# One Trainium2 core, two-layer decoder: the head of the program in another order, with constant products while memory is loaded

## The chip, the cores and the metric

The kernel runs on one core of one Trainium2 chip. The metric is the device time of one execution in microseconds (us). The engines are TensorE (PE, its weight loads listed apart as PEld), VectorE (DVE), ScalarE (ACT), GpSimd (POOL) and SyncE (SP), which issues most of the transfers.

## The reference

Two decoder layers over 1024 positions of width 1024, then a final norm. Layer 0 mixes with latent attention (`mla_mixer`), layer 1 with a sliding window (`swa_mixer`). In both, four memory heads run beside the mixer. What the head of the program computes of this is cut out here:

```python
mem_n = rmsnorm(mem, mem_norm_g)                  # mem: 256 x 1024
kv = (mem_n @ w_mem_kv[i])                        # both layers i, 1024 x 512 each
hn = rmsnorm(x, attn_norm_g[0])                   # x: 1024 x 1024
proj = hn @ w_in                                  # 1024 x 928: c_q 384, c_kv 256, k_r 32, q_cross 256
c_q, c_kv = rmsnorm(c_q, ...), rmsnorm(c_kv, ...)
k_rope = rope(k_r, positions)                     # sines and cosines of positions
```

## The kernel before

Every f32 product is made of three products of rounded halves: `split` (L96) writes the high part on ScalarE (`AF.Copy`, L99, or with a gain as scale, L102) and the rest on VectorE (L100 or L103), and a product of `a` and `b` is `ah*bh + ah*bl + al*bh`. So each tile that TensorE uses has passed through ScalarE and then VectorE.

The head, in the order of the text (L503 to L665):

- The two tiles of `mem` (128 x 1024 each, 512 KB) are loaded first on SyncE (L510), then `w_mem_kv` of both layers in four chunks each (`wm0`, `wm1`, L329), then x tiles 0 and 1 (L533), `w_in` in eight row blocks (L563) and further x tiles.
- `mem_T` (L464) transposes memory on TensorE (`psTm`, L473) and splits it into `memTh`, `memTl`. A `between` call puts the copy of the memory gains (`gcol`, L166) between the two tiles.
- `MemProj.mul(c)` (L331) splits one chunk of a layer's weights (`wmh`, `wml`) and multiplies it: 12 products of 128 x 512 (L342 to L344) into `psmk`, 48 for each layer.
- `mem_root` (L477) computes the norm factors of a memory tile: a square with sum on ScalarE (L179), a square root (L187), and one Newton step of five small VectorE operations (L188 to L192).
- `a_N(t)` does the same for x tile t, multiplies it by its factor into one of two places of `fa0` (called y0, y1, y2 below; L209), and issues the load of x tile t+2 into the place that this frees. `a_T(t)` transposes y (`psT_a`, L216) and splits it into `xhls`.
- `w_in` is split into `wih` and `wil` (128 x 928, eight times).
- `rope_tables` (L236) computes the angles on VectorE (tiles `rt`), two Sins on ScalarE (L289, L291), and `cosb` on VectorE (L292, L293).
- The loop at L639 then runs over the eight x tiles: transpose of tile k, norm of k+1, input projection of k-1 (`a_in`, tile `psin`, 48 products: eight steps of six, L117 to L120), transposes of the result of k-2 (`a_cT`, `psct`, L631 and L632).

`a_in` reads its PSUM tile with seven operations: two squares, three scaled copies (L619 to L621), and the four multiplies of `rope` (L308 to L311) that need the sine and cosine tables. The `psin` tiles have two PSUM buffers, so `psin2` is written into the one that `psin0` used.

Which instruction comes next on an engine is set at build time by a scheduler that follows priorities, the dependences and its own costs. On the chip each engine runs its row in order. `tc.issue_after(i)`, which the change uses, keeps what stands under it from being put into a row before instruction i.

## Time and profile before

| what | value |
|---|---|
| runs | 2111.02, 2110.83, 2110.26 us; median 2110.83 |
| profiled execution | 2109.36 us, of it the span 2107.5 us |
| TensorE busy | 2082.1 us (99% of the span) |
| VectorE, ScalarE busy | 1476.6 us (70%), 1114.6 us (53%) |
| TensorE's waits in the first 200 us | 4.6 us for memory, 1.8 for `wml`, 0.6 for y2, some smaller |

A line of the timeline gives the start within the span, the duration, the engine, the line of the kernel, the operation, its output and inputs by name (numbers left out), their shapes and the count of like instructions that were joined. What stands in brackets is the idle time of the engine before it, and what ended it. "SPq" is a transfer issued by SyncE. Records of neighbouring products overlap: the pace is the difference of two starts, not the duration of one.

### The profile page before, as it was taken

The page shows a single profiled execution, that of the slowest core. Times are in us where ns is not written, and L with a number is a line of the kernel's source. Part 1 is how long each engine was busy: PE and PEld are TensorE (multiplying, and loading weights), DVE is VectorE, ACT ScalarE, POOL GpSimd, SP SyncE. Part 2 cuts the span into 40 slices and gives each one's busy share as a digit, 9 for nine tenths or more (in the row PEclk, how much of TensorE's full clock was granted, in tenths as well). Part 3 has the DMA queues.
Part 4 walks back from the last instruction along what each step waited for, and adds up shares of the span by engine and source line. Part 5 has one row for each costly group of instructions (what it writes and reads, how often), then busy time and mean ns, then how long its engine had stood idle before and what let it go on. Part 6 is the DMA issues. An engine that isn't in the chain of part 4 may idle for free.

```text
span 2107.5 us, 28961 instructions
## 1 busy us (share of the span) xinstructions
PE 2082.1 (99%) x9830; PEld 1691.0 (80%) x9830; DVE 1476.6 (70%) x2929; ACT 1114.6 (53%) x2408; POOL 147.9 (7%) x248
## 2 busy tenths in 40 slices
PE   8999999999999999999999999999999999999998
PEld 7888766678888888888888878778788888888887
DVE  8766677775977776976557535666977776976565
ACT  7554466656755444444445435776755444444453
POOL 1001001010000000000001133420000000000000
PEclk9999999999999999999999999999999999999999
DMA  6202223343355446954433634542345446844342
GB/s 237 79 1 76 63 64 92 91 136 100 112 169 165 152 143 231 321 152 156 136 119 103 153 90 126 140 136 85 111 164 165 159 141 231 318 150 154 119 120 88
DMA packets 180756, 292.34 MB, mean 139 GB/s; under 512 B 16659, under 2 KB 70784, under 8 KB 180608
## 3 DMA queue, kind: packets, MB, share of 16 engines
q1 hardware_dynamic: 174096, 272.07, 41.4%
q0 software_dynamic: 5200, 15.80, 2.1%
q10 hardware_dynamic: 1312, 2.63, 0.4%
q8 instruction: 77, 1.26, 0.3%
q14 instruction: 71, 0.58, 0.1%
HBM read 187.34 MB, written 81.18 MB: 127 GB/s over the span
## 4 chain that ended last, share of the span: by engine, by line
PE 90%; DVE 5%; DMA 2%; ACT 2%; issue 1%; SPq 0%; DVEq 0%; ACTq 0%
PE psy L1730 5%; PE psy L1728 5%; PE psy L1729 5%; PE psu L1421 5%; PE psu L1422 5%; PE psu L1423 5%; PE psz L1728 4%; PE psz L1730 4%; PE psz L1729 4%; PE psv L1422 4%; PE psv L1421 4%; PE psv L1423 4%; PE pso L947 4%; PE pss L917 3%; PE pswo L108 3%; PE pswo L110 3%
## 5 line engine op out<-in xcount | busy, mean ns | idle before, releaser
L927 ACT ACTIVATE p<-pss 128x512 f32<-128x512 f32 (+2 forms) x144 | 68.7, 487 | 69.2 <-DVE pss L925 52.5
L1728 PE MATMUL psy<-g 128*128 128x512 f32 x256 | 99.9, 390 | 0.0
L1729 PE MATMUL psy<-g 128*128 128x512 f32 x256 | 99.6, 389 | 0.0
L1730 PE MATMUL psy<-g 128*128 128x512 f32 x256 | 99.4, 390 | 0.0
L99 ACT ACTIVATE g<-i 128x512 fp32r<-128x512 f32 x79 | 49.7, 629 | 92.5 <-PE psz L1729 46.0
L100 DVE TENSOR_TENSOR g<-i,g 128x512 fp32r<-128x512 f32 x79 | 55.6, 704 | 47.6 <-ACT g L99 47.6
L99 ACT ACTIVATE i<-mr 128x512 fp32r<-128x512 f32 x78 | 47.8, 628 | 74.0 <-PE psy L1729 25.6
L796 DVE TENSOR_REDUCE m<-psx 128x1 f32<-128x1024 f32 (+7 forms) x96 | 72.0, 752 | 20.1 <-PE psx L795 19.7
L99 ACT ACTIVATE uh<-i 128x512 fp32r<-128x512 f32 x66 | 41.7, 631 | 83.9 <-PE psy L1729 39.5
L947 PE MATMUL pso<-p,vf 128*128 128x512 f32 (+2 forms) x192 | 85.4, 527 | 0.6 <-ACT p L927 0.6
L100 DVE TENSOR_TENSOR uh<-i,uh 128x512 fp32r<-128x512 f32 x66 | 45.6, 690 | 46.8 <-ACT uh L99 46.6
L1728 PE MATMUL psz<-g 128*128 128x512 f32 x192 | 74.7, 389 | 0.0
L1729 PE MATMUL psz<-g 128*128 128x512 f32 x192 | 74.7, 389 | 0.0
L1730 PE MATMUL psz<-g 128*128 128x512 f32 x192 | 74.7, 389 | 0.0
L1320 ACT ACTIVATE mr<-mr,gcol 128x256 f32<-128x256 f32 (+1 forms) x160 | 63.9, 475 | 13.5 <-DMA mr<-in_mlp_w_up_dram 13.5
L100 DVE TENSOR_TENSOR i<-mr,i 128x512 fp32r<-128x512 f32 x78 | 53.6, 687 | 21.5 <-ACT i L99 21.5
L917 PE MATMUL pss<-qh,kh 97*128 97x512 f32 (+2 forms) x144 | 67.9, 474 | 0.0
L917 PE MATMUL pss<-ql,kh 97*128 97x512 f32 (+2 forms) x144 | 58.2, 404 | 0.0
L1641 DVE TENSOR_TENSOR mqf<-mqq,mqf 128x512 f32<-128x512 f32 x64 | 43.4, 688 | 20.6 <-DMA mqq<-in_mlp_w_down_dram 20.3
L1730 PEld LDWEIGHTS psy<-g 128*128 128x128 f32 x256 | 48.1, 188 | 10.0
L1729 PEld LDWEIGHTS psy<-g 128*128 128x128 f32 x256 | 48.1, 188 | 9.9
L1728 PEld LDWEIGHTS psy<-g 128*128 128x128 f32 x256 | 48.1, 188 | 9.8
(658 smaller groups left out, 6862.2 us busy)
## 6 DMA issues: line engine op xcount, KB each, us to landing
i<-hd SPq DMA_DIRECT2D x154, 256.0 KB
hd<-uh SPq DMA_DIRECT2D x76, 256.0 KB
hd<-ul SPq DMA_DIRECT2D x76, 256.0 KB
mr<-in_mlp_w_up_dram SPq DMA_DIRECT2D x36, 512.0 KB
hd<-x SPq DMA_DIRECT2D x72, 256.0 KB
mr<-hd SPq DMA_DIRECT2D x70, 256.0 KB
d<-in_mlp_w_up_dram SPq DMA_DIRECT2D x32, 512.0 KB
mqq<-in_mlp_w_down_dram SPq DMA_DIRECT2D x32, 512.0 KB
```

The lines of the kernel that those rows point to most:

```text
L99: nc.scalar.activation(hi, src, AF.Copy)
L100: nc.vector.tensor_tensor(lo, src, f32(hi), ALU.subtract)
L796: nc.vector.reduce_max(m8s[h][:, i : i + 1], ps[:, :n], axis=AX, negate=True)
L917: return lambda: nc.tensor.matmul(o, a, b, skip_group_check=True, **kw)
L927: nc.scalar.activation(p[:, c0:], ps, AF.Exp, scale=SC)
L947: mms.append(lambda: nc.tensor.matmul(o, a, b, skip_group_check=True, **kw))
L1421: nc.tensor.matmul(ps, wh[:, k, :], xh[:, k, :], start=p in (1, 2, 5) and k == 0, stop=False, skip_group_check=True)
L1422: nc.tensor.matmul(ps, wh[:, k, :], xl[:, k, :], start=False, stop=False, skip_group_check=True)
L1423: nc.tensor.matmul(ps, wl[:, k, :], xh[:, k, :], start=False, stop=k == 3, skip_group_check=True)
L1728: nc.tensor.matmul(ps, ah[:, j, :], bh, start=p in (1, 5, 2) and k == 0, stop=False, skip_group_check=True)
L1729: nc.tensor.matmul(ps, ah[:, j, :], bl, start=False, stop=False, skip_group_check=True)
L1730: nc.tensor.matmul(ps, al[:, j, :], bh, start=False, stop=k == NP - 1, skip_group_check=True)
```

## The change

The head's text is put in another order, with these parts:

- Eight products of a constant bf16 tile (`pswarm`), which nothing reads, stand ahead of all other TensorE work; the constant is written into a part of `f1` by VectorE.
- Loads: memory, the four chunks of `wm0`, two of `wm1`, x tile 0, the third chunk of `wm1`, x tile 1, the last chunk, then `w_in`.
- The gains of memory are copied ahead of the transposes of both memory tiles. The norm factors of both memory tiles are computed in one call (`mem_root`, width 2), behind the splits of layer 0's third chunk. Those of x tiles 0 and 1 share one Newton step too (`a_N(0, 2)`).
- All four chunks of layer 1 are multiplied in one loop. The splits of `w_in` come in a loop behind it, the first two held until layer 1's last split and y0, the others until the splits of x tile 0's transposes.
- `rope_tables` is held until the last split of `w_in`.

```diff
@@ -96,11 +96,12 @@
     def split(src, hi, lo, scale=None):
 
         if scale is None:
-            nc.scalar.activation(hi, src, AF.Copy)
-            nc.vector.tensor_tensor(lo, src, f32(hi), ALU.subtract)
+            a = nc.scalar.activation(hi, src, AF.Copy)
+            d = nc.vector.tensor_tensor(lo, src, f32(hi), ALU.subtract)
         else:
-            nc.scalar.activation(hi, src, AF.Copy, scale=scale)
-            nc.vector.scalar_tensor_tensor(lo, src, scale, f32(hi), ALU.mult, ALU.subtract)
+            a = nc.scalar.activation(hi, src, AF.Copy, scale=scale)
+            d = nc.vector.scalar_tensor_tensor(lo, src, scale, f32(hi), ALU.mult, ALU.subtract)
+        return a.ins, d.ins
 
     def mm3(ps, terms, first=True, last=True):
         n = len(terms)
@@ -214,7 +215,8 @@
             ps = ps1(f"psT_{name}_{a}")
             for i in range(4):
                 nc.tensor.transpose(ps[:, i * P : (i + 1) * P], y[:, (a + i) * P : (a + i + 1) * P], ident)
-            split(ps.rearrange("p (k c) -> p k c", k=4), *part(a))
+            last = split(ps.rearrange("p (k c) -> p k c", k=4), *part(a))
+        return last
 
 
     cosb = const.tile([P, NT, 16], F32, name="cosb")
@@ -323,10 +325,9 @@
         def __init__(self, layer, pl, src):
             self.layer, self.pl, self.src = layer, pl, src
 
-        def load(self):
+        def load(self, c):
             wsrc = w_mem_kv[self.layer].rearrange("(k p) n -> p k n", p=P)
-            for c, raw in enumerate(self.src):
-                nc.sync.dma_start(out=raw, in_=wsrc[:, 2 * c : 2 * c + 2, :])
+            nc.sync.dma_start(out=self.src[c], in_=wsrc[:, 2 * c : 2 * c + 2, :])
 
         def mul(self, c):
 
@@ -336,12 +337,12 @@
             th, tl = memT
             for i in range(2):
                 kt = 2 * c + i
-                split(self.src[c][:, i, :], w[0][:, i, :], w[1][:, i, :], scale=g_mem[:, kt : kt + 1])
+                self.done = split(self.src[c][:, i, :], w[0][:, i, :], w[1][:, i, :], scale=g_mem[:, kt : kt + 1])
                 for t in range(2):
                     o, ts = self.ps[:, t * 512 : t * 512 + 512], slice(t * P, (t + 1) * P)
                     nc.tensor.matmul(o, th[:, kt, ts], w[0][:, i, :], start=kt == 0, stop=False)
                     nc.tensor.matmul(o, th[:, kt, ts], w[1][:, i, :], start=False, stop=False)
-                    nc.tensor.matmul(o, tl[:, kt, ts], w[0][:, i, :], start=False, stop=kt == KT - 1)
+                    self.mm = nc.tensor.matmul(o, tl[:, kt, ts], w[0][:, i, :], start=False, stop=kt == KT - 1).ins
 
         def scaled(self, kv):
             self.kt = []
@@ -461,24 +462,22 @@
             nc.vector.tensor_scalar(p[:, h * 256 : (h + 1) * 256], p[:, h * 256 : (h + 1) * 256], rc[:, h : h + 1], None, ALU.mult)
         return p
 
-    def mem_T(pl, between):
-
-        mT = [pl.tile([P, KT, 256], F32R, name=f"memT{e}") for e in "hl"]
+    def mem_T(pl):
+
+        mT, hs = [pl.tile([P, KT, 256], F32R, name=f"memT{e}") for e in "hl"], []
         for t in range(2):
-            if t:
-                between()
             for a in range(0, KT, 4):
                 ps = ps1(f"psTm{t}_{a}")
                 for i in range(4):
                     nc.tensor.transpose(ps[:, i * P : (i + 1) * P], mxs[t][:, (a + i) * P : (a + i + 1) * P], ident)
-                split(ps.rearrange("p (k c) -> p k c", k=4), *[m[:, a : a + 4, t * P : (t + 1) * P] for m in mT])
-        return mT
-
-    def mem_root(pl, t):
-        r = pl.tile([P, 1], F32, name=f"mrs{t}")
-        rs = rstd_of(pl, [(mxs[t], D)], wms[0][:, 1, :] if t else fa0[:, 2, :])
-        nc.vector.tensor_copy(r, rs[:, 0:1])
-        return r
+                hs.append(split(ps.rearrange("p (k c) -> p k c", k=4), *[m[:, a : a + 4, t * P : (t + 1) * P] for m in mT]))
+        return mT, hs
+
+    def mem_root(pl):
+        r = pl.tile([P, 2], F32, name="mrs")
+        rs = rstd_of(pl, [(mxs[t], D) for t in range(2)], fa0[:, 2, :])
+        nc.vector.tensor_copy(r, rs)
+        return r[:, 0:1], r[:, 1:2]
 
     def kv_tiles(pl, layer):
         kv = MemKV()
@@ -499,6 +498,11 @@
         return quad.tile(shape, F32, tag="raw", bufs=2, name=name)
 
     fa0, f1 = quad_tile("f0", "fa0"), quad_tile("f1", "fa1")
+    nc.vector.memset(f1[:, 0, 0:256], 1.0)
+    warm = f1[:, 0, 0:256].bitcast(BF16)
+    wps = ps1("pswarm")
+    for _ in range(8):
+        nc.tensor.matmul(wps, warm[:, 0:P], warm, start=True, stop=True)
     xq = pool("xq", "right")
     kv0 = MemKV()
     kv0.kh, kv0.kl = [quad.tile([P, 4, 256], F32R, tag="raw", bufs=2, name=f"km{e}0") for e in "hl"]
@@ -512,60 +516,79 @@
     for layer in range(2):
         wms.append(quad_tile(f"q{layer}", f"wm{layer}"))
         mp.append(MemProj(layer, pm, [wms[layer][:, c, :].rearrange("p (k n) -> p k n", k=2) for c in range(4)]))
-    for m_ in mp:
-        m_.load()
-    mem_gains, rest_gains = gains(pm)
-    nc.scalar.activation(padl[:, 0:1], eps_t, AF.Sqrt)
-    memT = mem_T(pm, mem_gains)
-    small_loads()
-    for c in range(4):
-        mp[0].mul(c)
-        if c == 1:
-            rest_gains()
-    mem_rs = [mem_root(pm, t) for t in range(2)]
-    kvt = kv_tiles(pm, 1)
-    pa = pool("pa")
-    xts = []
-    xT, cs_ = {}, {}
-
     def load_x(t):
         xt = fa0[:, t % 2, :]
         nc.sync.dma_start(out=xt, in_=x[t * P : (t + 1) * P, :])
         return xt
 
-    xts = [load_x(0), load_x(1)]
+    xts = []
+    for c in range(4):
+        mp[0].load(c)
+    for c in range(4):
+        mp[1].load(c)
+        if c in (1, 2):
+            xts.append(load_x(c - 1))
+    mem_gains, rest_gains = gains(pm)
+    nc.scalar.activation(padl[:, 0:1], eps_t, AF.Sqrt)
+    mem_gains()
+    memT, mem_h = mem_T(pm)
+    small_loads()
+    for c in range(4):
+        with tc.issue_after(mem_h[1][0]):
+            mp[0].mul(c)
+        if c == 1:
+            with tc.issue_after(mp[0].mm):
+                rest_gains()
+        if c == 2:
+            with tc.issue_after(mp[0].done[0]):
+                mem_rs = mem_root(pm)
+    kvt = kv_tiles(pm, 1)
+    pa = pool("pa")
+    xT, cs_ = {}, {}
     xhls = quad_tile("q0", "xhls", F32R)
 
-    def a_N(t):
-        norm_y(pa, xts[t], fa0[:, 2 + t % 2, :])
-        if t + 2 < NT:
-            xts.append(load_x(t + 2))
+    def a_N(t, n=1):
+        rs = rstd_of(pa, [(xts[t + i], D) for i in range(n)], fa0[:, 2 + t % 2, :])
+        for i in range(n):
+            y = nc.vector.tensor_scalar(fa0[:, 2 + (t + i) % 2, :], xts[t + i], rs[:, i : i + 1], None, ALU.mult)
+            if t + i + 2 < NT:
+                xts.append(load_x(t + i + 2))
+            yield y.ins
 
     def a_T(t):
         y = fa0[:, 2 + t % 2, :]
         xhl = [xhls[:, 2 * (t % 2) + i, :].rearrange("p (k c) -> p k c", k=KT) for i in range(2)]
         xh, xl = xhl
-        T_split(y, lambda a: (xh[:, a : a + 4], xl[:, a : a + 4]), f"a{t}")
         xT[t] = (xh, xl)
+        return T_split(y, lambda a: (xh[:, a : a + 4], xl[:, a : a + 4]), f"a{t}")
 
     wih = pa.tile([P, KT, MLA_IN], F32R, name="wih")
     wil = pa.tile([P, KT, MLA_IN], F32R, name="wil")
     for c in range(4):
         mp[1].mul(c)
-        if c < 2:
-            a_N(c)
-        else:
-            a_T(c - 2)
         if c == 0:
             mp[0].scaled(kv0)
-        for kt in (2 * c, 2 * c + 1):
-            raw = f1[:, kt % 4, 0:MLA_IN]
-            nc.sync.dma_start(out=raw, in_=mla_w_in[0, kt * P : (kt + 1) * P, :])
-            split(raw, wih[:, kt, :], wil[:, kt, :], scale=g_attn[0][:, kt : kt + 1])
+        if c == 1:
+            first_N = a_N(0, 2)
+            y0 = next(first_N)
+        if c == 2:
+            xh0 = a_T(0)
+    for kt in range(KT):
+        raw = f1[:, kt % 4, 0:MLA_IN]
+        nc.sync.dma_start(out=raw, in_=mla_w_in[0, kt * P : (kt + 1) * P, :])
+        with tc.issue_after(mp[1].done[0] if kt < 2 else xh0[0]), tc.issue_after(y0 if kt < 2 else xh0[1]):
+            w_done = split(raw, wih[:, kt, :], wil[:, kt, :], scale=g_attn[0][:, kt : kt + 1])
+        if kt == 2:
+            with tc.issue_after(w_done[1]):
+                for _ in first_N:
+                    pass
+        if kt == 5:
+            a_T(1)
     mp[1].scaled(kvt)
     mp[0].keys(kv0)
     mp[1].keys(kvt)
-    rope_tables(pm)
+    with tc.issue_after(w_done[1]):
+        rope_tables(pm)
     masks(pm)
 
     for h in range(H):
@@ -641,7 +664,7 @@
         if 1 < k < NT:
             a_T(k)
         if 0 < k < NT - 1:
-            a_N(k + 1)
+            next(a_N(k + 1))
         if 1 <= k <= NT:
             a_in(k - 1)
         if 3 <= k <= NT:
```

Lines above L100 move by one or two in the changed kernel, those of the head more (L209 becomes L553 for y0 to y7, L179 becomes L180, L289 becomes L291).

Three places show how the engines' rows move. ScalarE around the two Sins, before: `ss` and `zs` are norm sums, `fa0` holds the x tiles, `sinb` and `rt8` are the sine table and the half angle; the square of x tile 4 is the last row here.

```order
L179 ACTIVATE fa0_86,ss7_669<-fa0_86 128x1024
L179 ACTIVATE fa1_87,ss6_633<-psin0_584 128x256
L187 ACTIVATE ss6_633<-zs6_634 128x2
L187 ACTIVATE ss7_669<-zs7_670 128x1
L99 ACTIVATE xhls_265<-psT_a2_0_655 128x512
L289 ACT_TABLE_LOAD
L289 ACTIVATE sinb_75<-rt8_500 128x128
L291 ACTIVATE rt8_500<-rt8_500 128x128
L621 ACTIVATE fa1_87<-psin0_584 128x256
L99 ACTIVATE xhls_265<-psT_a2_4_662 128x512
L179 ACTIVATE fa1_87,ss8_731<-psin1_682 128x384
L179 ACTIVATE fa0_86,ss9_790<-fa0_86 128x1024
```

The same place after; the square of x tile 4 is the row with `ss7_780`:

```order
L180 ACTIVATE fa1_87,ss6_721<-psin1_672 128x384
L180 ACTIVATE fa1_87,ss6_721<-psin1_672 128x256
L99 ACTIVATE xhls_264<-psT_a2_0_645 128x512
L99 ACTIVATE xhls_264<-psT_a2_4_652 128x512
L644 ACTIVATE fa1_87<-psin0_574 128x256
L180 ACTIVATE fa0_86,ss7_780<-fa0_86 128x1024
L291 ACT_TABLE_LOAD
L291 ACTIVATE sinb_75<-rt8_490 128x128
L293 ACTIVATE rt8_490<-rt8_490 128x128
L188 ACT_TABLE_LOAD
L188 ACTIVATE ss6_721<-zs6_722 128x2
```

The square of x tile 4 has moved from behind both Sins to ahead of their table load, and the `qc` copy (L644, before L621) too.

VectorE from y1 on, before (`rs4_334` is the factor of x tile 1):

```order
L103 SCALAR_TENSOR_TENSOR wml1_2_350<-wm1_102,gcol_73,wmh1_2_349 128x512
L209 TENSOR_SCALAR fa0_86<-fa0_86,rs4_334 128x1024
L103 SCALAR_TENSOR_TENSOR wil_267<-fa1_87,gcol_73,wih_266 128x928 x2
L100 TENSOR_TENSOR xhls_265<-psT_a0_0_367,xhls_265 128x512
L100 TENSOR_TENSOR xhls_265<-psT_a0_4_374,xhls_265 128x512
L103 SCALAR_TENSOR_TENSOR wml1_3_388<-wm1_102,gcol_73,wmh1_3_387 128x512 x2
L100 TENSOR_TENSOR xhls_265<-psT_a1_0_405,xhls_265 128x512
L100 TENSOR_TENSOR xhls_265<-psT_a1_4_412,xhls_265 128x512
L103 SCALAR_TENSOR_TENSOR wil_267<-fa1_87,gcol_73,wih_266 128x928 x2
L350 TENSOR_SCALAR ktok1_0_425<-psmk1_268,mrs0_231 128x256
```

After, from y0 on (`rs2_316` holds the factors of x tiles 0 and 1):

```order
L553 TENSOR_SCALAR fa0_86<-fa0_86,rs2_316 128x1024
L103 SCALAR_TENSOR_TENSOR wil_266<-fa1_87,gcol_73,wih_265 128x928 x2
L100 TENSOR_TENSOR xhls_264<-psT_a0_0_343,xhls_264 128x512
L100 TENSOR_TENSOR xhls_264<-psT_a0_4_350,xhls_264 128x512
L103 SCALAR_TENSOR_TENSOR wil_266<-fa1_87,gcol_73,wih_265 128x928
L553 TENSOR_SCALAR fa0_86<-fa0_86,rs2_316 128x1024
L103 SCALAR_TENSOR_TENSOR wil_266<-fa1_87,gcol_73,wih_265 128x928 x3
L100 TENSOR_TENSOR xhls_264<-psT_a1_0_395,xhls_264 128x512
L100 TENSOR_TENSOR xhls_264<-psT_a1_4_402,xhls_264 128x512
L103 SCALAR_TENSOR_TENSOR wil_266<-fa1_87,gcol_73,wih_265 128x928
L351 TENSOR_SCALAR ktok1_0_415<-psmk1_267,mrs_225 128x256
L368 TENSOR_TENSOR kml0_102<-pskm0_421,kmh0_101 64x2x256
```

Before, four splits of layer 1 and two `wil` stood around the splits of the transposed tiles 0 and 1, and y1 ahead of both; now no split of layer 1 is left behind y0, six `wil` (five of them shown) and y1 come behind the first `xhls`.

TensorE around the transposes of x tile 0, before:

```order
L216 MATMUL psT_a0_0_367<-ident_63,fa0_86 128x128
L343 MATMUL psmk1_268<-wml1_2_350,memTh_119 128x512
L344 MATMUL psmk1_268<-wmh1_2_349,memTl_120 128x512
L342 MATMUL psmk1_268<-wmh1_2_349,memTh_119 128x512
L343 MATMUL psmk1_268<-wml1_2_350,memTh_119 128x512
L344 MATMUL psmk1_268<-wmh1_2_349,memTl_120 128x512
L216 MATMUL psT_a0_0_367<-ident_63,fa0_86 128x128 x3
L216 MATMUL psT_a0_4_374<-ident_63,fa0_86 128x128 x4
L342 MATMUL psmk1_268<-wmh1_3_387,memTh_119 128x512
L216 MATMUL psT_a1_0_405<-ident_63,fa0_86 128x128 x4
L216 MATMUL psT_a1_4_412<-ident_63,fa0_86 128x128 x4
L117 MATMUL psin0_584<-wih_266,xhls_265 128x512
```

After, where all but the last chunk of layer 1 (12 products) stands ahead of them:

```order
L343 MATMUL psmk1_267<-wmh1_2_325,memTh_134 128x512
L344 MATMUL psmk1_267<-wml1_2_326,memTh_134 128x512
L345 MATMUL psmk1_267<-wmh1_2_325,memTl_135 128x512
L217 MATMUL psT_a0_0_343<-ident_63,fa0_86 128x128 x4
L217 MATMUL psT_a0_4_350<-ident_63,fa0_86 128x128 x4
L343 MATMUL psmk1_267<-wmh1_3_357,memTh_134 128x512
```

The transposes of x tile 0 have moved from the middle of layer 1's third chunk to its end, and those of x tile 1 from ahead of `psin0` to behind its first step. Further on, those of x tile 2 have moved from ahead of the last two steps of `psin1` to behind them.

## The prediction, on record before the changed kernel ran

> **What bounds the kernel now.** I read the page first, then the table of stretches, TensorE's waits in the first 200 us, and the timeline around the last of them.
>
> ```profile
> PE 2082.1 (99%) x9830; PEld 1691.0 (80%) x9830; DVE 1476.6 (70%) x2929; ACT 1114.6 (53%) x2408; POOL 147.9 (7%) x248
> PE 90%; DVE 5%; DMA 2%; ACT 2%; issue 1%; SPq 0%; DVEq 0%; ACTq 0%
> ```
>
> TensorE is busy for 99% of the span and carries 90% of the chain that ended last. A change in the head can only matter through what TensorE does not fill there.
>
> ```profile
> 27.05:31.30 4.25, 2.49 (x10) 1.49 (x9) 4.25 (x10) 4.15 (x7) 0.00 (x0) 1.00 0.93 297
> 31.30:56.78 25.48, 24.83 (x129) 21.57 (x127) 24.87 (x92) 14.04 (x28) 0.00 (x0) 1.00 0.27 99
> 56.78:62.08 5.30, 5.06 (x32) 3.96 (x32) 5.08 (x24) 4.58 (x11) 0.14 (x1) 1.00 0.42 110
> 62.08:130.00 67.92, 67.92 (x360) 61.15 (x360) 42.89 (x163) 33.97 (x110) 2.67 (x14) 1.00 0.16 52
> ```
>
> Columns: stretch, length, busy time of PE, PEld, DVE, ACT, POOL, granted clock, DMA share, GB/s. Up to 62 us VectorE is as full as TensorE (4.25 of 4.25, 24.87 of 25.48, 5.08 of 5.30). From 62.08 on TensorE has no gap for 68 us while VectorE is 63% busy. So what the change does is read from one event, the start of the products that fill that stretch (psin2, the input projection of x tile 2): later or earlier there is later or earlier at the end, one for one.
>
> ```profile
> PE psTm L473 <- DMA mem<-in_mem_dram: 4.6, 1, 4.6
> PE psmk L343 <- DVE wml L103: 1.8, 2, 1.3
> PE psT_a L216 <- DVE fa L209: 0.6, 1, 0.6
> ```
>
> TensorE's waits (total, times, longest) are these 7.0 us. The first is the transfer of memory, which the change leaves first in its queue; the other two are VectorE's lateness.
>
> ```profile
> 55.98 0.75 DVE L209 TENSOR_SCALAR fa<-fa,rs 128x1024 f32<-128x1024 f32 x1
> 56.75 4.22 SPq L533 DMA_DIRECT2D fa<-in_x_dram  x2
> 58.09 1.28 ACT L289 ACT_TABLE_LOAD   x1
> 58.99 0.59 PE L120 MATMUL psin<-wih,xhls 128*128 128x512 f32 x2
> 59.38 0.31 ACT L289 ACTIVATE sinb<-rt 128x128 f32<-128x128 f32 x1
> 59.60 0.29 ACT L291 ACTIVATE rt<-rt 128x128 f32<-128x128 f32 x1
> 60.48 0.28 DVE L292 TENSOR_TENSOR rt<-rt 128x128 f32<-128x128 f32 x1
> 61.00 1.06 ACT L179 ACTIVATE fa<-fa 128x1024 f32<-128x1024 f32 x1
> 61.29 0.22 DVE L293 TENSOR_SCALAR cosb<-rt 128x128 f32<-128x128 f32 x1
> 61.80 0.17 DVE L311 TENSOR_TENSOR fa<-psin,cosb 128x16 f32<-128x16 f32 x1
> 62.01 0.50 PE L117 MATMUL psin<-wih,xhls 128*128 128x512 f32 x1
> ```
>
> psin1's last pair starts at 58.99; psin2's first product starts at 62.01, behind the last of the four rope multiplies (L308 to L311) that read psin0's buffer: with two buffers, psin2 takes psin0's. Those multiplies need the sine and cosine tables: two Sins on ScalarE behind a table load, then L292 and L293. This is the tie that holds after the change too; TensorE's earlier waits only matter if they reach it.
>
> **The change, part by part.** First the start.
>
> ```profile
> 0.81 0.86 SPq L510 DMA_DIRECT2D mem<-in_mem_dram  x2
> 4.54 1.06 ACT L179 ACTIVATE fa<-mem 128x1024 f32<-128x1024 f32 x1 [1.61 <-DMA mem<-in_mem_dram]
> 4.65 1.94 PE L473 MATMUL psTm<-ident,mem 128*128 128x128 f32 x8 [4.65 <-DMA mem<-in_mem_dram]
> 8.11 0.72 ACT L102 ACTIVATE wmh<-wm,gcol 128x512 fp32r<-128x512 f32 x1 [0.89 <-DVE gcol L166]
> 8.88 0.79 PE L342 MATMUL psmk<-wmh,memTh 128*128 128x512 f32 x1
> 12.30 0.40 PE L343 MATMUL psmk<-wml,memTh 128*128 128x512 f32 x1
> 23.65 0.39 PE L342 MATMUL psmk<-wmh,memTh 128*128 128x512 f32 x1
> ```
>
> The eight constant products sit in the 4.65 us in which TensorE waits for memory. At 0.43 us each (8.88 and the pace behind it: six products by 12.07, my upper price) they take 3.4 us and end before 4.65: cost 0. ScalarE loses the square of memory ahead of the transposes' split (4.54, 1.06 us), and the gain column is copied sooner, so the first wmh (8.11, which had waited 0.89 us for it) moves up by about 0.9 us and the first psmk product to about 8.0.
>
> In the new order 84 psmk products (48 of layer 0, 36 of layer 1) stand ahead of the first transposes of x (psT_a0); all are paced by TensorE: from 12.30 to 23.65 there are 50 of them, 0.227 us each. 84 x 0.227 = 19.1, with 0.8 us for the first splits: psT_a0 at 27.9. The two waits for wml at L343 (1.8 us) disappear, since VectorE no longer puts a w_in split ahead of them. Until psT_a0 VectorE has y0 and two wil to do, which it can finish about 1.8 us before it gets the transposed tile: that idle time is new.
>
> ```profile
> 32.76 1.09 ACT L99 ACTIVATE xhls<-psT_a 128x512 fp32r<-128x512 f32 x2 [0.71 <-PE psT_a L216]
> 30.84 0.74 DVE L209 TENSOR_SCALAR fa<-fa,rs 128x1024 f32<-128x1024 f32 x1
> 33.70 1.27 DVE L100 TENSOR_TENSOR xhls<-psT_a,xhls 128x512 fp32r<-128x512 f32 x2
> 34.90 1.40 DVE L103 SCALAR_TENSOR_TENSOR wml<-wm,gcol,wmh 128x512 fp32r<-128x512 f32 x2
> 31.50 2.27 DVE L103 SCALAR_TENSOR_TENSOR wil<-fa,gcol,wih 128x928 fp32r<-128x928 f32 x2
> ```
>
> Four transposes (0.5) and one ScalarE copy (half of 1.09) after 27.9, VectorE starts xhls of tile 0 at about 29.1. Before, from there (33.70) to y2, the norm of x tile 2 (55.98), it took 22.28 us with hardly a gap. After, the same stretch holds two wml less (-1.3), four wil more (two had been done after xhls before, six are left now: 4 x 1.1 = +4.4) and y1 more (+0.66, one of 30.84): 22.28 - 1.3 + 4.4 + 0.66 = 26.0. y2 then starts at 55.1 instead of 55.98, and ends at 55.8.
>
> TensorE meanwhile goes through: 27.9, 8 transposes (about 0.9), 12 psmk products (2.7), psT_a1 and the key transposes (16, 1.8), then 16 steps of the input projection:
>
> ```profile
> 45.08 0.39 PE L117 MATMUL psin<-wih,xhls 128*128 128x512 f32 x1
> 46.34 0.39 PE L117 MATMUL psin<-wih,xhls 128*128 128x512 f32 x1
> ```
>
> Six products per step, 1.26 us: 16 x 1.26 = 20.2. The sum is 53.5, say 53.9 with small stalls, for the end of psin1, against 59.6. So TensorE is **5.7 us ahead** there. It cannot keep it, since psin2 still waits for the rope multiplies.
>
> And these get later. The y2 operation frees its source buffer for x tile 4, whose load SyncE issues then (56.75 in the profile, right behind 55.98 + 0.75). The load of the first memory tile, of the same 512 KB, was issued at 0.81 and used at 4.54: 3.7 us; between 3.4 and 3.9 I take 3.5, so x4 lands at 55.8 + 3.5 = 59.3. In the new ScalarE order the square of x4 (its norm sum) stands **ahead** of the Sin table load; before it stood behind both Sins (61.00 against 58.09). ScalarE runs in order, so the tables wait for that transfer: square 1.05 to 60.4, table load 1.28 to 61.7, Sins 0.22 + 0.29 to 62.2, L292 and L293 0.3, and from L293's start to psin2 62.01 - 61.29 = 0.72: psin2 at 63.2 to 63.3 instead of 62.01: **+1.3 us**. Bounds: -0.7, if VectorE's 1.8 us of idle time didn't arise; +2.0, if the transfer takes 3.9 and y2 starts at 55.4.
>
> The clock of the start is a second term. Products ran at full pace from 12.07, 3.2 us after the first at 8.88; the six before took 3.2 us where 6 x 0.227 would do. If the constant products have TensorE at full pace by 8.0, psT_a0 comes at 27.9; if not, the same slow start costs up to 1.0 us more, and all behind moves with it. The nearest rows (transposes between 4.65 and 8.88 did not raise the pace; real products did) don't say whether products that end 3 us earlier hold it. Ends 0 and +1.0; half: **+0.5**.
>
> The third term is the clock after the new gap. Between psin1's end (53.9) and 63.3 TensorE has only 23 transposes, 9.4 us without a real product.
>
> ```profile
> 2099.49 0.39 PE L1730 MATMUL psy<-mqq,x 128*128 128x512 f32 x1
> 2104.30:2107.50 3.20, 0.00 (x0) 0.00 (x0) 0.00 (x0) 0.00 (x0) 0.00 (x0) 0.50 0.44 164
> ```
>
> The last product ended at 2099.9, and from 2104.30 the granted clock is 0.50: 4.4 us without work were enough to lose half. The longest pause between real products before is 2.4 us (59.6 to 62.0), and psin2 then ran at once at the full pace. At the start, transposes did not bring the pace up. So I expect psin2 to start at half pace, for 3.0 to 4.4 us (3.2 us at the start; 4.4 at the end of the run, the other way), with 0.465 of it lost (0.43 against 0.23 us per product): 1.4 to 2.0, **+1.7**. If transposes hold the clock, 0.
>
> [...]
>
> The rest at nothing. One Newton pass instead of two for memory and for x0 and x1 saves some ten operations of 0.15 us on VectorE, in the stretch in which it then idles. x0 and x1 load ahead of the last two chunks of wm1: those land about 2.6 us later, still before TensorE needs them (about 22 us; were they late, TensorE would stall in psmk and psT_a0 with it, one for one). The w_in splits come later; psin0 needs the first at 31.6, VectorE has two by 27.5 and one more every 1.1 to 1.5 us, under the 1.26 us of a step or near it. On SyncE one x load (tile 7) goes behind a weight load, far from the head.
>
> Sum: 1.3 + 0.5 + 1.7 = 3.5 us. The profiled execution took 2109.36 us (span 2107.5), 1.47 below the median of the runs, 2110.83. So 2112.9 for it, and **2114.3** on the median.
>
> **Rivals.**
> A, the clock holds: transposes count as work, or the pause is too short. For it: no pause of this length with transposes is in the trace. Then +1.3 + 0.5: 2112.6.
> C, not slower: the square of x4 doesn't hold the tables. The point is VectorE's start on xhls of tile 0: at 27.5 or before (no idle time), y2 starts 1.6 to 1.8 us sooner and psin2 at 61.4 to 61.6, 0.6 before now; with the clock held, 2110.2. Against it: the 84 products ahead, 19.1 us that nothing shortens.
> [...]
> That the change doesn't do what it says (the new orders unused) is excluded by the orders shown.
>
> **How the numbers follow.** Forecast 0.46 (2113.2 to 2115.2), A 0.25, C 0.12, D 0.17. A measurement can tell about 0.2%, 4.2 us, from no change: under 2106.6 or over 2115.05. Nothing here gives the first except an unseen gain, 0.04 out of C. Over it lies most of D (0.14) and the upper end of the forecast (0.12): 0.26. Within: 0.70. The range takes C's time and D's with its bound: 2110.0 to 2116.4.
>
> **What would show it.** Right: in the new profile TensorE's waits for wml gone; VectorE idle ahead of the first xhls; the square of x4 ahead of the table load and waiting for its transfer; a PE wait of some microseconds ahead of psT_a3 or psin2; psin2's first products 0.43 us apart. Wrong: psin2 before 62.0; the clock at full pace there; psT_a0 after 29; or psmk waiting for wm1.

## The result and the profile after

The changed kernel takes **2116.37 us** (median of 7 runs, 2113.14 to 2119.91), the kernel before 2110.51 us beside it (7 runs, 2108.90 to 2111.02). The ratio is 1.0030, 95% interval 1.0020 to 1.0039: about 6 us slower. The profiled execution took 2118.11 us, with a span of 2116.2 us. A second set of runs (11, under e5 below) gave 2115.88 us and a ratio of 1.0025 (1.0016 to 1.0034).

TensorE's share and the chain that ended last look as before on the page:

```profile
PE 2088.3 (99%) x9838; PEld 1693.8 (80%) x9838; DVE 1474.3 (70%) x2919; ACT 1114.7 (53%) x2406; POOL 148.5 (7%) x248
PE 89%; DVE 6%; DMA 2%; ACT 2%; issue 1%; SPq 0%; DVEq 0%; ACTq 0%
```

TensorE's busy time has grown by 6.2 us (2082.1 to 2088.3), of which the constant products are 3.4. The other 2.8 us are the same products as before, which took longer at a lower clock (granted 0.996 of full speed on the mean, 0.999 in the trace of before). TensorE's waits in the first 200 us (total, times, longest) are other ones than before:

```profile
PE psT_a L217 <- DVE rt L247: 2.4, 1, 2.4
PE psT_a L217 <- DVE zs L181: 2.4, 1, 2.4
PE psmk L343 <- ACT wmh L102: 2.1, 1, 2.1
PE psin L118 <- DVE fa L313: 1.4, 1, 1.4
```

The wait for memory (4.6) and that for `wml` (1.8) have shrunk to 0.3 us each, as forecast (TensorE first waits 1.3 us for the constant tile). In their place it waits for y2 and y3 (the first two lines; the view names another small VectorE operation beside them), for the first weights, and for the rope multiplies. The timeline around the last of these, after:

```profile
58.73 0.75 DVE L553 TENSOR_SCALAR fa<-fa,rs 128x1024 f32<-128x1024 f32 x1
59.51 5.20 SPq L521 DMA_DIRECT2D fa<-in_x_dram  x2
62.70 0.22 DVE L290 TENSOR_SCALAR rt<-rt 128x128 f32<-128x128 f32 x1
62.89 1.06 ACT L180 ACTIVATE fa<-fa 128x1024 f32<-128x1024 f32 x1 [1.23 <-DMA fa<-in_x_dram]
64.06 1.28 ACT L291 ACT_TABLE_LOAD   x1
64.50 1.06 PE L217 MATMUL psT_a<-ident,fa 128*128 128x128 f32 x8 [2.35 <-DVE zs L181]
66.73 0.17 DVE L313 TENSOR_TENSOR fa<-psin,cosb 128x16 f32<-128x16 f32 x1
66.95 0.80 PE L118 MATMUL psin<-wih,xhls 128*128 128x512 f32 x1 [1.39 <-DVE fa L313]
```

This is the forecast chain, link by link: y2, then the load of x tile 4, its square on ScalarE (which waits for that load), the table load, the Sins, the rope multiplies, psin2. One link that the forecast did not have stands just behind it: the transposes of x tile 3 (64.50) are ahead of psin2 on TensorE and wait for y3, so the rope multiplies are the last of two waits, by 1.39 us. The chain stands 3.6 us later than forecast: y2 at 58.73 instead of 55.1, psin2 at 66.95 instead of 63.3. And psin2's first product takes 0.80 us instead of 0.50. The stretches show the clock (columns as in the prediction):

```profile
11.00:14.30 3.30, 3.30 (x9) 2.20 (x8) 3.30 (x6) 3.30 (x7) 0.26 (x1) 0.52 1.04 374
54.00:64.00 10.00, 5.43 (x31) 4.19 (x29) 9.86 (x51) 3.53 (x9) 0.00 (x0) 1.00 0.19 74
67.00:72.00 5.00, 5.00 (x14) 4.21 (x15) 4.08 (x14) 4.60 (x14) 0.28 (x2) 0.50 0.32 121
455.00:458.20 3.20, 3.20 (x9) 2.40 (x8) 3.07 (x9) 1.73 (x3) 0.00 (x0) 0.50 0.46 173
```

From 54 to 64 us TensorE is half idle while VectorE works 9.86 of 10 us. From about 65.7 to 72.6 the granted clock is 0.50. It is also 0.50 at two places that the prediction did not have: from about 11.1 to 14.5, under the first psmk products, and from 454.9 to 458.3, in the output projection of layer 0. Setting TensorE's products of the two traces side by side, the distance is 4.94 us at psin2's start, 7.46 us at 72.7, 7.6 us ahead of the stretch at 455 and 9.2 us behind it, and 8.7 us at the end. So of this execution's 8.75 us, 4.9 are psin2's start, 2.5 the half clock behind it, and about 1.6 the one at 455, of which later stretches give some 0.5 back.

### The profile page after: what moved, and what is told of

Read it like the earlier page. It is cut to its first block, busy times and chain, and to the rows that moved or that the text cites. A ratio compares the mean times of both kernels' runs of the same rounds, so it can differ in the third digit from the quotient of the medians.

```text
span 2116.2 us, 28971 instructions
## 1 busy us (share of the span) xinstructions
PE 2088.3 (99%) x9838; PEld 1693.8 (80%) x9838; DVE 1474.3 (70%) x2919; ACT 1114.7 (53%) x2406; POOL 148.5 (7%) x248
## 3 DMA queue, kind: packets, MB, share of 16 engines
q8 instruction: 77, 1.26, 0.2%
## 4 chain that ended last, share of the span: by engine, by line
PE 89%; DVE 6%; DMA 2%; ACT 2%; issue 1%; SPq 0%; DVEq 0%; ACTq 0%
PE psy L1753 5%; PE psy L1751 5%; PE psy L1752 5%; PE psu L1444 5%; PE psu L1445 5%; PE psu L1446 5%; PE psz L1752 4%; PE psz L1753 4%; PE psz L1751 4%; PE psv L1444 4%; PE psv L1445 4%; PE psv L1446 4%; PE pso L970 3%; PE pss L940 3%; PE pswo L109 2%; PE pswo L111 2%
## 5 line engine op out<-in xcount | busy, mean ns | idle before, releaser
L100 DVE TENSOR_TENSOR g<-i,g 128x512 fp32r<-128x512 f32 x79 | 55.4, 701 | 46.9 <-ACT g L99 46.9
L100 DVE TENSOR_TENSOR uh<-i,uh 128x512 fp32r<-128x512 f32 x66 | 45.5, 689 | 45.3 <-ACT uh L99 45.3
L100 DVE TENSOR_TENSOR i<-mr,i 128x512 fp32r<-128x512 f32 x78 | 53.5, 686 | 20.7 <-ACT i L99 20.7
```

Source lines behind the costliest of these rows:

```text
L100: d = nc.vector.tensor_tensor(lo, src, f32(hi), ALU.subtract)
```

## The experiments

All times are medians of 11 runs, beside 33 runs of the kernel before on the same chip. The experiments ran on three chips (e1 to e4, e5 to e8, e9 to e12); the kernel before took 2110.79, 2110.60 and 2110.55 us there, so that times can be compared across them to about 0.2 us. The places are starts in each kernel's own trace, us:

| kernel | psT_a0 | first xhls | y2 | psin2 | median | ratio to before, 95% |
|---|---|---|---|---|---|---|
| before | 29.42 | 33.70 | 55.98 | 62.01 | | |
| changed | 31.11 | 32.38 | 58.73 | 66.95 | 2116.37 (7 runs) | 1.0020 to 1.0039 |
| e1, no constant products | 28.97 | 30.24 | 57.04 | 65.30 | 2115.24 | 1.0014 to 1.0032 |
| e2, Sins ahead of the square | 28.70 | 29.96 | 57.14 | 63.72 | 2113.16 | 1.0002 to 1.0020 |
| e3, e2 and filled pause | 29.40 | 30.67 | 57.43 | 64.08 | 2111.48 | 0.9997 to 1.0015 |
| e4, transposes a chunk earlier | 26.50 | 28.46 | 55.55 | 61.64 | 2110.36 | 0.9989 to 1.0007 |
| e5, changed again | 28.84 | 30.11 | 57.06 | 65.21 | 2115.88 | 1.0016 to 1.0034 |
| e6, old middle loop | 28.10 | 30.24 | 55.48 | 62.02 | 2111.95 | 1.0000 to 1.0018 |
| e7, rope columns copied | 29.16 | 30.42 | 56.98 | 60.29 | 2110.25 | 0.9991 to 1.0009 |
| e8, e4 and e7 | 27.39 | 29.35 | 56.08 | 60.57 | 2108.88 | 0.9983 to 1.0000 |
| e9, e8 with Sins behind the copies | 26.78 | 28.74 | 56.03 | 59.74 | 2108.92 | 0.9983 to 1.0001 |
| e10, before, copies as in e9 | 31.38 | 35.66 | 57.91 | 62.04 | 2109.88 | 0.9990 to 1.0007 |
| e11, before and constant products | 29.72 | 33.99 | 56.25 | 62.28 | 2111.15 | 0.9995 to 1.0012 |
| e12, before and new loads | 32.38 | 34.45 | 57.59 | 64.11 | 2110.29 | 0.9991 to 1.0008 |

The theory ("theory 1" below) after the result: the time is lost because VectorE's chain to y2 and to the sine tables starts late, and because the clock falls in the pause which that leaves TensorE.

### e1: without the constant products

```diff
-    nc.vector.memset(f1[:, 0, 0:256], 1.0)
-    warm = f1[:, 0, 0:256].bitcast(BF16)
-    wps = ps1("pswarm")
-    for _ in range(8):
-        nc.tensor.matmul(wps, warm[:, 0:P], warm, start=True, stop=True)
```

> The change without its eight constant products and their memset. Theory 1 (what costs is where VectorE's chain starts, and the half clock after the long pause): the first psmk products then run at half pace from their start at about 9 us, instead of at half pace from 11.1 to 14.3 as in the changed kernel; either way about 1.6 us are lost, so the time stays within 1 us of the changed kernel's 2116.4. Rival 1 (the constant products themselves cost, since the clock falls under the psmk products behind them): psT_a0 comes at 29.5 instead of 31.1, and the time falls by 1.6 to about 2114.8.

Measured: 2115.24, between the two forecasts and, against e5's 2115.88, no difference that these runs can tell. The constant products neither cause the loss nor cure it. In e1's trace psmk starts at 8.31 us and psT_a0 at 28.97. Its first products do not run at half pace, as theory 1 had it, although only transposes ran ahead of them: TensorE did 21 operations from 10 to 15 us, as many as in e12, whose products start 0.23 us apart there (18 in the kernel before, 14 in the changed kernel's first trace). The half pace between 11 and 14.5 us is not there either (clock 1.00), nor in e5's trace (1.00), which has the constant products. It stands in one of the two traces of the changed kernel, behind TensorE's 2.07 us of waiting for late first weights.

### e2 and e3: the Sins first, and the pause filled

```diff
+            if k == 3:
+                with tc.issue_after(sin_b):
+                    next(a_N(k + 1))
```

(`sin_b` is the second Sin; x tile 4's square can't stand ahead of it.) e3 adds products of `wih` with itself, ten behind psin1 and eight behind psct, which nothing reads (and issues psin1's products apart from the operations that read them, so that the first ten can stand between):

```diff
+        for i in range(n):
+            nc.tensor.matmul(o, wih[:, 0, 0:P], wih[:, 0, 0:512], start=i == 0, stop=i == n - 1)
```

> The change with the square of x tile 4 held behind the two Sins on ScalarE. Theory 1: the tables were ready for the Sins when VectorE finished the angles (62.9), and the square with its wait for the transfer held the table load until 64.06: psin2 starts 1.1 us earlier, at 65.8 instead of 66.95, the half clock after the pause stays (5 us of it): 2115.2. Rival 2 (the square's wait is what the change lost, as the prediction's first term had it): nearly the whole 4.9 us come back, psin2 at 62 to 63, 2112.

> As e2_sines_first, with 18 products that nothing reads in TensorE's pause: ten behind psin1, eight behind the psct transposes. Theory 1: psin2 starts as in e2_sines_first (65.8) but at full pace, 0.23 us from product to product, and 2.5 us or more are won on it: 2112.6. Rival (the half pace after the pause has nothing to do with the pause, or short fillings do not hold the clock): the products behind 66 us are still 0.43 us apart, and the time is that of e2_sines_first.

e2 gives 2113.16, 2.7 us under e5, more than theory 1's 1.2 but far from "nearly the whole". From the first xhls to psin2 it takes 33.76 us (changed: 34.57 and 35.10), so the order of the square against the Sins is worth 0.8 to 1.3 us in the traces. It can't be worth more while the row of TensorE stays: in e2 psin2 (63.72) follows directly on the transposes of x tile 3 (62.90), which waited 2.36 us for y3. What the rest of the 2.7 us is, no run here separates. e3 gives 2111.48, 1.7 us less than e2 with the same order on ScalarE. The granted clock of the two, e2 first:

```profile
56.00:63.70 7.70, 2.96 (x23) 2.41 (x23) 7.49 (x37) 5.73 (x13) 0.06 (x1) 1.00 0.21 68
64.60:67.60 3.00, 3.00 (x10) 2.66 (x9) 2.86 (x9) 2.84 (x8) 0.00 (x0) 0.50 0.78 303
```

```profile
56.00:64.00 8.00, 7.07 (x40) 5.36 (x39) 7.65 (x39) 5.42 (x11) 0.20 (x2) 1.00 0.24 69
64.00:68.00 4.00, 4.00 (x22) 3.56 (x21) 3.53 (x12) 3.94 (x11) 0.20 (x2) 1.00 0.68 258
```

In e2 TensorE has 2.96 us of work (transposes) in the 7.7 us ahead of psin2, and the clock falls to 0.50 under psin2 for 3 us: 10 products in it, where e3 has 22 in 4 us. In e3 it is busy for 7.07 of 8 us, and the clock stays at 1.00. psin2 itself starts no earlier. So in e2 the pause costs the half clock, and the half clock 1.6 us (worked out from the two traces: two steps of psin2 take 4.36 us in e2 and 2.75 in e3).

### e4: the transposes of x tile 0 one chunk earlier

```diff
         if c == 1:
             first_N = a_N(0, 2)
             y0 = next(first_N)
-        if c == 2:
             xh0 = a_T(0)
```

> The change with the transposes of x tile 0 issued one chunk earlier, so that 24 psmk products stand behind them instead of 12 (the Sins then also stand ahead of the square of x tile 4). Theory 1: VectorE's 2.6 us of idle time ahead of the first xhls go, y2 comes at 56.2 instead of 58.7, and psin2 at about 63.3: 2113 with the half clock that stays. Rival 3 (VectorE waits for w_in's transfers or for splits of layer 1 instead): y2 not earlier than 58, time as in e2_sines_first, 2115.

2110.36: the whole loss is gone, 5.5 us against e5, by one line. VectorE at that place, first in e5 and then in e4:

```profile
26.34 2.27 DVE L103 SCALAR_TENSOR_TENSOR wil<-fa,gcol,wih 128x928 fp32r<-128x928 f32 x2
30.11 1.29 DVE L100 TENSOR_TENSOR xhls<-psT_a,xhls 128x512 fp32r<-128x512 f32 x2 [1.49 <-ACT xhls L99]
```

```profile
26.27 2.27 DVE L103 SCALAR_TENSOR_TENSOR wil<-fa,gcol,wih 128x928 fp32r<-128x928 f32 x2
28.46 1.28 DVE L100 TENSOR_TENSOR xhls<-psT_a,xhls 128x512 fp32r<-128x512 f32 x2
```

Up to 28.6 us the two are alike; then VectorE stands idle for 1.49 us in e5 (2.56 in the changed kernel's first trace) and goes on at once in e4. y2 comes 1.5 us earlier, the scheduler puts the Sins ahead of the square again, psin2 comes 3.6 us earlier, and the clock stays at 1.00 under it (TensorE busy for 3.50 of 4.60 us ahead of psin2). y2 at 55.55 and psin2 at 61.64 are better than I expected of it. The one line thus moved several rows at once (the transposes of x tile 2 are also back inside psin1); how the 5.5 us divide among VectorE's idle time, the Sins' place and the clock is not separated.

### e5: the changed kernel again

> The changed kernel once more, for a second trace beside its first and a median on the same chip as the runs below. Theory 1: psT_a0 near 29 as in e1 to e3 where the weights land in time, and psin2 36 us behind it, near 65; then half pace for 3 to 6 us; median 2115 to 2117. If the first trace is typical instead, psT_a0 at 31 again, with the half pace at 11 to 14 us.

Its trace is of its fastest execution (2112.92). TensorE, from psin1's last products on:

```profile
55.02 0.58 PE L121 MATMUL psin<-wih,xhls 128*128 128x512 f32 x2
57.94 1.94 PE L217 MATMUL psT_a<-ident,fa 128*128 128x128 f32 x8 [2.34 <-DVE rt L247]
59.68 1.77 PE L654 MATMUL psct<-ident,fa 128*128 128x128 f32 x7
63.28 1.07 PE L217 MATMUL psT_a<-ident,fa 128*128 128x128 f32 x8 [1.84 <-DVE zs L181]
65.21 0.79 PE L118 MATMUL psin<-wih,xhls 128*128 128x512 f32 x1 [0.86 <-DVE fa L313]
67.91 0.46 PE L118 MATMUL psin<-wih,xhls 128*128 128x512 f32 x1
```

psT_a0 stands at 28.84 and psin2 at 65.21, as expected; so 31.11 and 66.95 in the first trace were a late execution. Behind psin1 the clock fell to 0.50 within 2.3 us: eight transposes take 1.94 us at 57.94 and 1.07 us at 63.28. Half pace under psin2 lasted 2.8 us here and cost 1.2 us.

### e6: the old middle loop with the new start

```diff
-        if c == 1:
-            first_N = a_N(0, 2)
-            y0 = next(first_N)
-        if c == 2:
-            xh0 = a_T(0)
-    for kt in range(KT):
...
+        if c < 2:
+            next(a_N(c))
+        else:
+            a_T(c - 2)
+        for kt in (2 * c, 2 * c + 1):
...
+    rope_tables(pm)
```

> The changed kernel with the middle loop of before (norms, transposes and splits of w_in between the chunks of layer 1, no gates, rope tables not held), but with the new start: constant products, new load order, shared norm step of memory. Theory 1 (the new middle is what costs): psin2 back at 61 to 62.5 as before, full pace there, time within 1 us of before's 2110.8. Rival 4 (the new start costs: x loaded ahead of layer 1's weights): psin2 stays after 64, 2114 or more.

2111.95, psin2 at 62.02 with the clock at 1.00: the new middle loop costs about 4 us of the 5.3, which leaves about 1.3 for the new start. The interval of e6 (0.0 to 1.8 thousandths, 0 to 3.8 us) leaves open whether the start costs anything; e11 and e12 ask for two of its parts.

### e7, e8 and e9: without the tie between psin2 and the tables

```diff
-        rope(pa, ps[:, 640:672].rearrange("p (h c) -> p h c", h=1), c[:, CKR : CKR + 32]...
+        kr = f1[:, t % 2, MLA_IN + 32 : MLA_IN + 64]
+        nc.scalar.activation(kr, ps[:, 640:672], AF.Copy)
+        rope(pa, kr.rearrange("p (h c) -> p h c", h=1), c[:, CKR : CKR + 32]...
```

e8 adds e4's line; e9 also writes the reduced angle to `sinb`, and issues both Sins behind the copy of the first tile:

```diff
+        copied = nc.scalar.activation(kr, ps[:, 640:672], AF.Copy).ins
+        with tc.issue_after(copied):
+            for _ in tables:
+                pass
```

> The changed kernel, with the 32 columns that rope reads copied from PSUM to SBUF by ScalarE, so that psin2 no longer waits for the sine tables. Theory 1 (VectorE's chain to y2 comes first, the tables second): psin2 starts behind the copies, some 5 us ahead of the changed kernel (61.5 to 62 where that had 66.95, 60 to 60.5 where it had 65.3), the pause of TensorE shrinks to under 6 us and costs less half pace; 2110 to 2111. Rival (the buffer is not what psin2 waits for, but the splits of x tile 2): psin2 less than 1.5 us earlier, 2114.

> The transposes of x tile 0 one chunk earlier (as e4_early_transposes) and the copy of the rope columns (as e7_copy_kr) together. Theory 1: psin2 starts behind the copy, which stands behind the Sins on ScalarE: 60.0 instead of 61.64 in e4_early_transposes, 2108.7. If the splits of x tile 2 or the rope result inside psin2 hold it instead: 2110, as e4_early_transposes.

> As e8_early_and_copy, with the Sins issued behind the copies on ScalarE (the table load too), so that neither the tables nor their load stand between y2 and psin2. Theory 1: psin2 comes behind VectorE's scaled copies of psin0 and the psct transposes, at about 59 instead of 60.57, and the pause ahead of it is too short for the clock to fall: 2107.5, under before's 2110.7. If the splits of x tile 2 hold psin2 instead: 2108.9 as e8_early_and_copy.

e7 gives 2110.25: a 0.2 us copy takes psin2 from 65.2 to 60.29, although y2 is as late as in e5 (56.98) and the square still stands ahead of the Sins. ScalarE in e7:

```profile
59.51 0.39 ACT L644 ACTIVATE fa<-psin 128x256 f32<-128x256 f32 x1
59.77 0.22 ACT L646 ACTIVATE fa<-psin 128x32 f32<-128x32 f32 x1
61.04 1.06 ACT L180 ACTIVATE fa<-fa 128x1024 f32<-128x1024 f32 x1 [1.05 <-DMA fa<-in_x_dram]
62.21 1.28 ACT L291 ACT_TABLE_LOAD   x1
63.51 0.31 ACT L291 ACTIVATE sinb<-rt 128x128 f32<-128x128 f32 x1
```

and TensorE:

```profile
60.29 0.78 PE L118 MATMUL psin<-wih,xhls 128*128 128x512 f32 x1
64.00 1.04 PE L217 MATMUL psT_a<-ident,fa 128*128 128x128 f32 x8
```

The square still waits for x tile 4 and the Sins come at 63.51, but psin2 has been running since 60.29 (its first 2 us at a clock of 0.50). So it need not wait for the table chain, as the prediction said. But the copy did two things: with the tie gone, the scheduler also put psin2 ahead of the transposes of x tile 3 (64.00), which stood ahead of it in e5 (63.28). In e5 psin2 waited only 0.86 us for the rope multiplies once these transposes were done (1.39 in the first trace). So the copy without the new row could have won about that much; the 4.9 us need both. e8 (2108.88) and e9 (2108.92) are the fastest here, 1.6 to 1.7 us under the kernel before in the median, at the edge of what these runs can tell (interval 0.9983 to 1.0000 and 1.0001). e9's tables come later than e8's (Sin at 60.9 against 59.55) and psin2 0.8 us earlier, but the time is the same; my 2107.5 was too low.

### e10, e11 and e12: parts on the kernel before

e10 is e9's copy and order in the kernel before, e11 the constant products alone (the lines of e1 put in), e12 the order of loads alone:

```diff
-    for m_ in mp:
-        m_.load()
+    for c in range(4):
+        mp[0].load(c)
+    for c in range(4):
+        mp[1].load(c)
+        if c in (1, 2):
+            xts.append(load_x(c - 1))
```

> The kernel before with the same copy of the rope columns and the Sins behind it; nothing of the change. Theory 1: psin1 ends at 59.6, the seven psct transposes follow, psin2 at 60.4 instead of 62.0, so 2109.2; e9_early_copy_ahead stays ahead of it, since its VectorE chain is earlier. If the change's parts gave nothing even so, both would have the same time.

> The kernel before with the eight constant products alone. Theory 1: they bring the first psmk products to full pace, up to 1.8 us of it, but VectorE is the bound from 21 us on, so that psin2 moves by under 0.5 us: 2110.2 to 2111. Rival 1: the clock falls again a few us later (as it did at 11 to 14 us in the first trace of the changed kernel) and the time rises by 1 or more.

> The kernel before with the new order of loads alone (x tiles 0 and 1 ahead of the last two chunks of layer 1's weights). Theory 1: neither x nor these chunks are waited for by TensorE, psin2 within 0.5 us of 62.0: 2110.2 to 2111.2. Rival 4 (layer 1's chunks come late): a wait for weights in psmk, psin2 1 us or more later, 2112.

None of the three differs from the kernel before by what can be told (2109.88, 2111.15, 2110.29). e10's trace is of a late execution (first psmk product at 9.33, psin2 at 62.04), so that the 1.6 us that I expected stand neither shown nor refuted. e11 is inconclusive for the same size; its trace has full pace from the first psmk products on (0.23 us apart from 10.13) and no fall of the clock behind it (1.00 from 10 to 15 us), against rival 1. e12's trace contradicts what I expected of it: psin2 at 64.11 instead of within 0.5 us of 62.0, behind a longer wait for a split of layer 1 (2.8 us, 1.3 before), while its median does not show it; one trace is not enough to say how often this happens.

## Why the prediction fell short, step by step

- **What bounds it, right.** psin2's start carried the result; TensorE had no gap behind it:

```profile
70.00:130.00 60.00, 60.00 (x317) 54.06 (x316) 37.55 (x141) 28.52 (x94) 2.01 (x10) 0.98 0.14 43
```

- **Constant products, right in cost.** They ran from 1.26 to 4.65 us, 3.39 us, as priced, ahead of the transposes of memory. Their use was priced as half of 1.0 us; e1 and e11 show none, and e1's first products were at full pace without them (21 operations from 10 to 15 us, as many as in e5 with them).
- **The start, wrong in size: this is the first half of the step that failed.** "The first psmk product to about 8.0" came at 8.17 in e5 and at 9.21 in the first trace, where the first weights arrived late (`wmh` at 8.44, 1.93 us of wait for its transfer). "psT_a0 at 27.9" came at 28.84 and 31.11 (after 29 was named as a sign of being wrong). From first product to psT_a0 e5 needs 20.7 us, of which 19.1 are 84 products: 1.6 us of slow beginnings and waits where the sum had 0.8. The first trace has the half clock from 11.1 to 14.5 on top. So the start made psin2 later by 0.9 us in a good execution and 3.2 in a bad one, where the sum had +0.5. (The lower bound that the prediction gives for psin2, -0.7, does not come out of its own numbers: 1.3 less 1.8 is -0.5.)
- **VectorE from the first xhls to y2, 26.0, short: the second half.** It took 26.95 us in e5 and 26.35 in the first trace. In e5 busy time was 25.35, near the 26.0 that was counted; the rest is waiting, 1.3 us of it for `wih`, whose raw rows came late (ScalarE waited 1.4 us for w_in's transfer). The later splits of w_in, priced at nothing, are these.

```profile
30.10:57.06 26.96, 24.83 (x124) 21.18 (x122) 25.35 (x92) 17.33 (x34) 0.00 (x0) 1.00 0.35 129
```

- **From y2 to psin2, right.** In the first trace the load of x tile 4 was issued at 59.51 and used at 62.89, 3.4 us (forecast 3.5); from there to psin2 it took 4.06 us (forecast 3.9 to 4.0). The square ahead of the Sins does wait. What the prediction did not see is that y3 and its transposes hold psin2 to within 0.9 to 1.4 us of the same place, so that little is won where the tables alone come sooner (e2). Together psin2 came 3.2 (e5) to 4.9 us late instead of 1.3 + 0.5 = 1.8.
- **The clock behind the pause: size near, reason only in part.** +1.7 was forecast; it cost 1.2 in e5, 2.5 in the first trace, 1.6 to 1.7 between e2 and e3. But it was priced on a pause that began with psin1's last product, as if transposes let the clock fall. In the first trace that product ends at 57.3, and the clock is still 1.00 at 65.7. From 58.92 to 62.33 transposes alone kept TensorE busy for 2.16 of 3.41 us, and the clock stayed at 1.00 behind them; from 62.33 to 65.75 they kept it busy for 1.06 us, and from there it was 0.50. So the clock held for a time with transposes alone, as rival A had it, and fell where fewer of them ran. That the price came out near the measured ones is in part luck. Worked out from the clock of stretches of 1 or 0.5 us, half pace lasts from 57.8 to 61.2 in e5, and from 11.1 to 14.5 and 454.9 to 458.3 in the first trace, 3.4 us each, and twice that, 65.7 to 72.6, behind the pause.
- **The sum.** 1.3 + 0.5 + 1.7 = 3.5 was forecast; the medians differ by 5.3 (e5) and 5.9 us. The chain to psin2 was the one forecast; the start and the w_in waits ahead of it were mis-sized, by 0.4 and 0.95 us in e5 and by 2.7 and 0.35 in the first trace. That took the time from 3.5 us past the 4.2 us (0.2%) to which the prediction gave a chance of 0.26; as the intervals begin at 1.0020 and 1.0016, that border itself is reached and not clearly passed. e5's traced execution, 3.6 us over that of the kernel before, meets the sum by luck: its parts are 3.2 and 1.2 instead of 1.8 and 1.7, and later stretches give 0.9 back.
- **The rivals.** A (the clock holds) is refuted in its result: the clock is 0.50 under psin2 in both traces of the changed kernel; in e3, with the pause filled (7.07 of 8 us busy), it was 1.00. C (VectorE starts its xhls at 27.5) is refuted by all traces of the changed kernel; e4 shows that C's condition was nearly what an order one chunk earlier gives (28.46), and its time is that of no change. D (half pace for 3.4 us more than forecast, 2115.9) has the measured time, but by luck: no trace had shown those 3.4 us when D was priced, the first trace had 6.8 us of half clock, e5 only 2.8 under psin2, and D had psT_a0 at 27.9.

What stays open: how the 6 to 7 us of spread between single executions of the changed kernel divide between late first weights and half-clock stretches (no trace of it is of an execution near the median: 2112.92 is the lowest of its 11, 2118.11 the second highest of its 7); and whether the new start alone costs up to 1.3 us (e6).

## What to carry to other kernels

Giving an engine that isn't the bound a smooth row (TensorE without its waits, 2.3 to 4.0 us ahead at psin1's end: its last pair starts at 56.68 and 55.02, before at 58.99) is worth nothing if the bounding engine then stands idle: look at what VectorE waits for in the new order, since its idle time here came back at the next tie. And look for the tie itself, and for the next one behind it; a 0.2 us copy that frees a PSUM buffer from a late table, with the new row of TensorE that came with it, did as much as the best reordering (2110.25 against 2110.36). A pause of TensorE cost more than its length where the clock fell to 0.50 behind it: 1.2 us more in e5, 2.5 in the first trace.

## What the runs showed of the hardware

- The clock fell after a shorter stop than the 4.4 us seen at the end of the kernel before: in e5 it is 0.50 from 57.8 on, behind 2.3 us without any product.
- It also fell behind waits of 0.41 us at most. In the first trace of the changed kernel TensorE was busy for 4.13 of the 5 us up to 455.0, and the clock still fell for 3.4 us; at the same place (440 to 447 us, 5.63 of 7) it did not in the kernel before:

```profile
440.00:447.00 7.00, 5.63 (x28) 3.46 (x26) 6.81 (x15) 5.79 (x16) 0.00 (x0) 1.00 0.96 311
450.00:455.00 5.00, 4.13 (x18) 2.27 (x16) 4.81 (x10) 4.17 (x13) 0.00 (x0) 0.99 0.93 335
```

- Of fourteen traces, this stretch near 450 us appears in the changed kernel's first and in those of e8, e10 and e12 (mean clock 0.93 from 440 to 465 us, 1.00 in the other ten), and costs about 1.6 us in the first. The changed kernel's own two traces differ in it (e5 has none), so executions of the same code differ by that much.
- In the first trace the moments at which the granted clock changes lie whole multiples of 3.41 us apart (11.13, 14.55, 65.75, 72.57, 454.87 and 458.28). In other traces half clock near psin2 lasted 3.4 us in e2 (from 64.3), e5 (from 57.8 and from 64.6) and e7 (from 58.8), and 10.2 us in e1 (from 58.5), so where it lies differs between executions. In the 3.41 us ahead of these falls near psin2 TensorE was busy for 31 to 42% of the time (1.06 us in the first trace, 1.43 in e2); near there the clock held behind 47% (e2, 1.60 us up to 57.50) and 63% (first trace, 2.16 us up to 62.33). That is no rule for the whole kernel: ahead of the fall at 454.87 it was 2.61 of 3.41 us, 76%.
- In e5 the clock rose with transposes alone. Nothing but the 15 transposes of 57.94 and 59.68 ran between 55.6 and 63.28, and the clock, 0.51 from 58.0 to 61.3, was back at 1.00 from 61.5:

```profile
58.00:61.30 3.30, 3.30 (x15) 2.84 (x15) 2.97 (x8) 1.62 (x4) 0.00 (x0) 0.51 0.48 159
61.50:63.30 1.80, 0.02 (x1) 0.05 (x1) 1.59 (x10) 1.78 (x3) 0.00 (x0) 1.00 0.00 0
```

The prediction had read the start of the kernel before as showing the opposite. The start goes both ways: with little but transposes ahead of them, the first psmk products were at full pace in e1 and e12 (21 operations each from 10 to 15 us; in e12 the products start 0.23 us apart from 10.05 on) and at half pace in the kernel before (0.43 us apart up to 11.73), and e10 had 14 operations from 10 to 15 us. With the clock at 1.00, eight f32 transposes took 1.07 us in e5 (63.28), beside the 1.94 us at 57.94 with the clock at 0.50.
